# The residual of the last column group is put into PSUM ahead of the tail's matmuls

## The chip, the cores and the metric

The kernel runs on one core of a Trainium2 chip. The metric is the device time in microseconds (us) of one execution. Engines: PE is the matmul engine, DVE the vector engine, ACT the scalar engine, POOL the general one, SP the engine that issues most DMAs. [...]

## What is computed

A trunk of two layers over 256 tokens of width 2048 in float32: gated linear attention, then retention, each with a pre-norm, a SiLU gate, an output projection and a residual add, and a final norm. What matters here is the end: the output projection of the second layer, the residual add and the final norm.

```python
def rms_norm(x, g):
    xf = x.astype(jnp.float32)
    xn = xf * lax.rsqrt(jnp.mean(xf * xf, axis=-1, keepdims=True) + EPS)
    return xn.astype(x.dtype) * g

def reference(...):
    h = x
    for i in range(DEPTH):                       # DEPTH = 2
        ...
            h = h + gla_mixer(rms_norm(h, gla_norm[j]), ...)
        ...
            h = h + retention_mixer(rms_norm(h, ret_norm[j]), ...)   # ends in (o * silu(gate)) @ w_out
    return rms_norm(h, final_norm)
```

## The kernel before

The tokens are two tiles of 128 (t = 0, 1), the 2048 output columns four groups of 512. The weights stream from HBM in blocks of 256 rows by 512 columns (`raw`). Each block is split into a high and a low part (`hi` by ACT at L298, `lo` by DVE at L299), and a float32 product is made of three matmuls (high by high, high by low, low by high): the `mm3` helper, L340 to L342. A projection group is a loop over row blocks that accumulates into one PSUM bank per token tile.

The second half of the last output projection is written out by hand in `out_last` and `out_tail`. Column group 0 comes first. Of group 3 the first four row blocks are done early (`HEAD = 4`), and their sum is added to the residual tile `resid` in SBUF. Then `out_pair` does groups 1 and 2 together, in a scheme with fewer products; its banks are called `rbe_ps`, and its results are joined into `resid` by DVE (`join`, L990 and L992), squared and summed by ACT (`square_sum`, L599) and multiplied by the final norm's weights by DVE (L1005). What is left for `out_tail` is the other four row blocks of group 3, for which the weights are already split and kept.

`out_tail` goes over the token tiles. For tile 0 it issues 24 matmuls of 512 columns into one bank (`tail_ps`). For tile 1 it issues 48 of 256 columns into two banks, so that the first half of the columns is done before the second. Behind each tile stands its epilogue, in halves of 256 columns: DVE adds the PSUM result to the residual (L1150), ACT squares it and sums the squares (L1152), DVE multiplies it by the norm weights (L1154). Then a short chain of small operations (`rsqrt_col`, L1115 to L1120) gives the token's factor, DVE and ACT scale the five column pieces by it (L1168, L1170), and each piece is sent out by a DMA (L1172), issued on SP's queue after a DVE scaling and on ACT's own queue after an ACT scaling.

The order on an engine is set by a scheduler at build time, from data dependences and an estimate of times. `keep(...)` pins an instruction behind the instruction that was traced just before it on the same engine (an ordering, no wait for its end). The last splits, the joins, the squares of the joint pair and the table load at the start of `out_tail` (L1126) are pinned, and so are the tail's matmuls, as `mm3` pins every matmul of a group that does not begin at row block 0:

```python
        pin = keep if begin else lambda x: x
...
    keep(nc.scalar.preload_act_table_set("natural_log_exp_and_others"))
...
                eng = nc.scalar if which == "s" else nc.sync
                eng.dma_start(out[t * P : (t + 1) * P, piece], src)
```

PSUM banks for the accumulators go round in a queue of four (`slots`). When `out_tail` begins, its order is 1, 2, 3, 0: tile 0 gets bank 1, tile 1 banks 2 and 3.

## Time and profile before

| | |
|---|---|
| median of 3 runs | 1374.77 us (1374.18 to 1375.06) |
| profiled execution | 1373.6 us, its span 1371.8 us |
| PE busy | 1361.9 us, 99% of the span |
| DVE busy | 1100.0 us, 80% |
| ACT busy | 846.6 us, 62% |
| mean granted PE clock | 0.998 |

The span runs from the first to the last instruction of the profiled execution; what lies around it is in the time of the execution. A timeline row has the start in us from the span's start, the duration, the engine and the line of the kernel, the operation, "out<-in" by the program's names, the shape, and in brackets how long the engine had been idle before it and what ended that. Matmuls are pipelined: their starts are the reliable column, and the end of a matmul is modelled.

### The profile page before, as it was taken

The page shows a single profiled execution, that of the slowest core. Times are in us where ns is not written, and L with a number is a line of the kernel's source. Part 1 is how long each engine was busy: PE and PEld are TensorE (multiplying, and loading weights), DVE is VectorE, ACT ScalarE, POOL GpSimd, SP SyncE. Part 2 cuts the span into 40 slices and gives each one's busy share as a digit, 9 for nine tenths or more (in the row PEclk, how much of TensorE's full clock was granted, in tenths as well). Part 3 has the DMA queues.
Part 4 walks back from the last instruction along what each step waited for, and adds up shares of the span by engine and source line. Part 5 has one row for each costly group of instructions (what it writes and reads, how often), then busy time and mean ns, then how long its engine had stood idle before and what let it go on. Part 6 is the DMA issues. An engine that isn't in the chain of part 4 may idle for free.

```text
span 1371.8 us, 18375 instructions
## 1 busy us (share of the span) xinstructions
PE 1361.9 (99%) x6564; PEld 1143.5 (83%) x6564; DVE 1100.0 (80%) x1524; ACT 846.6 (62%) x1116; POOL 136.7 (10%) x194
## 2 busy tenths in 40 slices
PE   9999999999999999999999999999999999999997
PEld 8888888888888888888888888888888888888886
DVE  7686795987878896769888888887867897889796
ACT  6576656656567747656666566655546666666565
POOL 1003020110021021001011010100101101010010
PEclk9999999999999999999999999999999999999999
DMA  9755566789658667868897878896798797869773
GB/s 365 257 172 167 174 203 184 158 249 324 192 153 268 205 205 180 314 168 239 271 321 201 256 202 252 207 313 215 174 363 230 234 262 195 262 194 321 236 179 121
DMA packets 84507, 315.03 MB, mean 230 GB/s; under 512 B 9776, under 2 KB 10800, under 8 KB 83136
## 3 DMA queue, kind: packets, MB, share of 16 engines
q1 hardware_dynamic: 67200, 241.63, 50.6%
q0 software_dynamic: 15920, 64.89, 23.7%
q10 hardware_dynamic: 1296, 7.35, 1.5%
q8 instruction: 51, 0.84, 0.2%
q14 instruction: 40, 0.33, 0.1%
HBM read 303.35 MB, written 10.49 MB: 229 GB/s over the span
## 4 chain that ended last, share of the span: by engine, by line
PE 96%; DMA 2%; DVE 1%; issue 1%; ACT 0%; DVEq 0%; POOL 0%; ACTq 0%; POOLq 0%
PE rqk_ps L383 8%; PE re_ps L412 7%; PE re_ps L413 7%; PE re_ps L411 7%; PE rqk_ps L384 4%; PE gqk_ps L383 4%; PE gg_ps L341 3%; PE gv_ps L342 3%; PE gv_ps L341 3%; PE gv_ps L340 3%; PE gg_ps L342 3%; PE gg_ps L340 3%; PE ge_ps L413 2%; PE ge_ps L411 2%; PE ge_ps L412 2%; PE gae_ps L413 2%
## 5 line engine op out<-in xcount | busy, mean ns | idle before, releaser
L299 DVE TENSOR_TENSOR lo<-raw,hi 128x1024 fp32r<-128x1024 f32 (+1 forms) x568 | 687.1, 1219 | 215.6 <-ACT hi L298 206.5
L298 ACT ACTIVATE hi<-raw 128x1024 fp32r<-128x1024 f32 (+1 forms) x568 | 596.1, 1055 | 393.8 <-PE gg_ps L342 49.0
L383 PE MATMUL rqk_ps<-xhl,hi 128*128 128x512 f32 x480 | 162.8, 397 | 0.0
L412 PE MATMUL re_ps<-lo,xhl 128*128 128x512 f32 x352 | 137.4, 390 | 0.3 <-DVE lo L299 0.3
L413 PE MATMUL re_ps<-hi,xhl 128*128 128x512 f32 x352 | 137.1, 390 | 0.0
L310 POOL DMA_DIRECT2D raw<-in_w_all x90 | 78.0, 868 | 555.4 <-DVE lo L299 270.6
L411 PE MATMUL re_ps<-hi,xhl 128*128 128x512 f32 x352 | 132.4, 391 | 0.0
L384 PE MATMUL rqk_ps<-xhl,lo 128*128 128x256 f32 x480 | 122.3, 280 | 0.0
L383 PEld LDWEIGHTS rqk_ps<-xhl,hi 128*128 128x128 f32 x480 | 89.5, 188 | 17.9
L384 PEld LDWEIGHTS rqk_ps<-xhl,lo 128*128 128x128 f32 x480 | 87.5, 189 | 3.4
L412 PEld LDWEIGHTS re_ps<-lo,xhl 128*128 128x128 f32 x352 | 66.1, 188 | 13.9 <-DVE lo L299 0.8
L413 PEld LDWEIGHTS re_ps<-hi,xhl 128*128 128x128 f32 x352 | 66.1, 188 | 13.7
L411 PEld LDWEIGHTS re_ps<-hi,xhl 128*128 128x128 f32 x352 | 66.0, 188 | 13.3
L383 PE MATMUL gqk_ps<-xhl,hi 128*128 128x512 f32 x216 | 76.6, 399 | 0.0
L341 PE MATMUL gg_ps<-lo,xhl 128*128 128x512 f32 x192 | 75.4, 393 | 0.0
L341 PE MATMUL gv_ps<-lo,xhl 128*128 128x512 f32 x192 | 75.2, 392 | 0.0
L340 PE MATMUL gv_ps<-hi,xhl 128*128 128x512 f32 x192 | 75.1, 393 | 0.0
L342 PE MATMUL gv_ps<-hi,xhl 128*128 128x512 f32 x192 | 75.0, 391 | 0.0
L342 PE MATMUL gg_ps<-hi,xhl 128*128 128x512 f32 x192 | 74.9, 390 | 0.0
L340 PE MATMUL gg_ps<-hi,xhl 128*128 128x512 f32 x192 | 74.8, 391 | 0.0
L828 POOL TENSOR_TENSOR s<-s,m 128x64 f32<-128x64 f32 x56 | 36.0, 674 | 232.6 <-DVE m L819 223.3
L384 PE MATMUL gqk_ps<-xhl,lo 128*128 128x256 f32 x216 | 59.0, 280 | 0.0
(434 smaller groups left out, 2654.8 us busy)
## 6 DMA issues: line engine op xcount, KB each, us to landing
raw<-in_w_all SPq DMA_DIRECT2D x449, 512.0 KB, 5.0
raw<-in_w_all POOLq DMA_DIRECT2D x90, 512.0 KB, 6.9
resid<-in_x_n SPq DMA_DIRECT2D x2, 1024.0 KB, 10.0
gg<-in_gn_g POOLq DMA_DIRECT2D x8, 256.0 KB, 4.4
resid_x<-resid ACTq DMA_DIRECT2D x1, 2048.0 KB, 7.9
gb<-in_gn_b POOLq DMA_DIRECT2D x8, 256.0 KB, 5.8
gb_resid<-resid_x POOLq DMA_DIRECT2D x1, 2048.0 KB, 11.1
resid_g<-gb_resid ACTq DMA_DIRECT2D x1, 2048.0 KB, 9.5
```

The lines of the kernel that those rows point to most:

```text
L298: a = nc.scalar.activation(hi[:, sl], src[:, sl], AF.Copy)
L299: b = nc.vector.tensor_tensor(lo[:, sl], src[:, sl], hi[:, sl].bitcast(F32), ALU.subtract)
L310: nc.gpsimd.dma_start(raws[n], block(key), accum_op=ALU.add)
L340: pin(mm(ps, xh, hi[:, q, :], start=kt == begin, stop=False))
L341: pin(mm(ps, xh, lo[:, q, :], start=False, stop=False))
L342: pin(mm(ps, xl, hi[:, q, :], start=False, stop=kt == end - 1))
L383: mm(ps[c], wh, rhs[:, kt, :, :], start=kt == 0, stop=False)
L384: mm(ps[c][:, 0, :], wl, rhs[:, kt, 0, :], start=False, stop=False)
L411: pin(mm(ps, xh, hi[:, q, :], start=start, stop=False, **again))
L412: pin(mm(ps, xh, lo[:, q, :], start=False, stop=False, **again))
L413: pin(mm(ps, xl, hi[:, q, :], start=False, stop=stop, **again))
L828: nc.gpsimd.tensor_tensor(dst, dst, side_of(m[:, li, :], z), ALU.add)
```

## The change

Ahead of each tile's matmuls, ACT copies the residual of the last column group into the banks that the matmuls will use: one copy of 512 columns for tile 0, two of 256 for tile 1, each pinned by `keep`. The first matmul of the group no longer overwrites the bank (`start` only where the row block is 0), so the matmuls add to what was copied. In the epilogue the add on DVE goes, and the square and the multiply read PSUM instead of the residual tile in SBUF. The copies are traced at L1135 of the new kernel; for tile 0 the instruction traced before them on ACT is the table load, for tile 1 it is the last output DMA that tile 0's epilogue issues on ACT's queue.

```diff
@@ mm3
         pin = keep if begin else lambda x: x
-        pin(mm(ps, xh, hi[:, q, :], start=kt == begin, stop=False))
-        pin(mm(ps, xh, lo[:, q, :], start=False, stop=False))
-        pin(mm(ps, xl, hi[:, q, :], start=False, stop=kt == end - 1))
+        onto = {"skip_group_check": True} if begin else {}
+        pin(mm(ps, xh, hi[:, q, :], start=kt == 0, stop=False, **onto))
+        pin(mm(ps, xh, lo[:, q, :], start=False, stop=False, **onto))
+        pin(mm(ps, xl, hi[:, q, :], start=False, stop=kt == end - 1, **onto))
@@ out_tail
             ps = acc(2, f"tail_ps{t}", (P, half)) if t else acc(1, f"tail_ps{t}")
+            for n, p in enumerate(ps):
+                w = half if t else GW
+                keep(nc.scalar.activation(p, cur["resid"][:, t, base + n * w : base + (n + 1) * w], AF.Copy))
             for j in range(HEAD, NSUB):
...
             for n in range(2):
-                dst = cur["resid"][:, t, base + n * half : base + (n + 1) * half]
-                nc.vector.tensor_tensor(dst, ps[n] if t else ps[0][:, n * half : (n + 1) * half], dst, ALU.add)
+                at = slice(n * half, (n + 1) * half)
+                src = ps[n] if t else ps[0][:, at]
                 junk = sg_p.tile([P, half], F32, tag="sg", name="sqj")
-                nc.scalar.activation(junk, dst, AF.Square, accum_out=sq[:, n : n + 1])
-                at = slice(n * half, (n + 1) * half)
-                nc.vector.tensor_tensor(last[:, at], dst, fns[3][:, at], ALU.mult)
+                nc.scalar.activation(junk, src, AF.Square, accum_out=sq[:, n : n + 1])
+                nc.vector.tensor_tensor(last[:, at], src, fns[3][:, at], ALU.mult)
```

## The prediction

> **What bounds the kernel now.** I read the page's head and the chain that ended last first, then the timeline of the last 32 us, because the edit touches nothing before that. "PE" is the matmul engine, "DVE" the vector engine, "ACT" the scalar engine.

> ```profile
> span 1371.8 us, 18375 instructions
> PE 1361.9 (99%) x6564; PEld 1143.5 (83%) x6564; DVE 1100.0 (80%) x1524; ACT 846.6 (62%) x1116; POOL 136.7 (10%) x194
> PE 96%; DMA 2%; DVE 1%; issue 1%; ACT 0%; DVEq 0%; POOL 0%; ACTq 0%; POOLq 0%
> ```

> PE is the bound: it is busy for 99% of the span and is 96% of the chain. ACT has slack (62%), but slack over the span says nothing of the moment at which the new copies run. That moment is in the next rows: the timeline (start, duration, engine, line) where the last joint pair of column groups (rbe_ps) ends and the tail (tail_ps) begins.

> ```profile
> 1352.01 0.39 PE L413 MATMUL rbe_ps<-hi,ogt 128*128 128x512 f32 x1
> 1352.24 0.39 PE L340 MATMUL tail_ps<-xhl,ogt 128*128 128x512 f32 x1
> 1352.26 0.68 DVE L990 TENSOR_TENSOR rb_resid<-rbe_ps,rb_resid 128x512 f32<-128x512 f32 x1
> 1353.04 0.63 ACT L599 ACTIVATE sqj<-rb_resid 128x512 f32<-128x512 f32 x1 [2.68 <-DVE rb_resid L990]
> 1353.79 0.69 DVE L1005 TENSOR_TENSOR rb_resid<-rb_resid,fn 128x512 f32<-128x512 f32 x1 [0.85 <-ACT sqj L599]
> 1354.40 0.68 DVE L990 TENSOR_TENSOR rb_resid<-rbe_ps,rb_resid 128x512 f32<-128x512 f32 x1
> 1355.18 0.63 ACT L599 ACTIVATE sqj<-rb_resid 128x512 f32<-128x512 f32 x1 [1.42 <-DVE pre L1129]
> 1355.72 0.19 ACT L599 ACTIVATION_READ_ACCUMULATOR sqj<-rb_resid 128x1 f32 x1
> 1355.92 1.28 ACT L1126 ACT_TABLE_LOAD   x1
> ```

> Two things are to be seen. PE goes from rbe_ps to tail_ps without a gap (1352.01 to 1352.24, the usual spacing). And ACT is behind it: joins on DVE, squares on ACT and multiplies on DVE wait for one another in turn, so ACT's last square ends at 1355.91 and its table load at 1357.20, when token tile 0's 24 tail matmuls are nearly all issued. Today nobody on PE waits for that.

> The end of token tile 0 and its epilogue, which today lies beside token tile 1's matmuls:

> ```profile
> 1357.45 0.39 PE L342 MATMUL tail_ps<-xhl,ogt 128*128 128x512 f32 x1
> 1357.68 0.28 PE L340 MATMUL tail_ps<-xhl,ogt 128*128 128x256 f32 x1
> 1357.88 0.75 DVE L1150 TENSOR_TENSOR rb_resid<-tail_ps,rb_resid 128x256 f32<-128x256 f32 x2 [1.00 <-PE tail_ps L342]
> 1358.40 0.42 ACT L1152 ACTIVATE sqj<-rb_resid 128x256 f32<-128x256 f32 x1 [1.19 <-DVE rb_resid L1150]
> 1358.55 0.75 DVE L1154 TENSOR_TENSOR last<-rb_resid,fn 128x256 f32<-128x256 f32 x2
> 1359.22 0.20 DVE L1156 TENSOR_SCALAR pre<-sq,pre 128x1 f32<-128x1 f32 x1
> 1359.52 0.29 ACT L1116 ACTIVATE nf_nw<-sq,pre 128x1 f32<-128x1 f32 x1 [0.21 <-DVE pre L1156]
> 1360.64 1.12 ACT L1170 ACTIVATE rb_resid<-rb_resid,fin 128x256 f32<-128x256 f32 x2 [0.59 <-DVE fin L1120]
> 1361.18 0.96 ACTq L1172 DMA_DIRECT2D out<-rb_resid  x2
> ```

> And the end of token tile 1, which sets the end of the kernel:

> ```profile
> 1363.31 0.28 PE L342 MATMUL tail_ps<-xhl,ogt 128*128 128x256 f32 x1
> 1363.71 0.42 DVE L1150 TENSOR_TENSOR rb_resid<-tail_ps,rb_resid 128x256 f32<-128x256 f32 x1
> 1364.16 0.42 ACT L1152 ACTIVATE sqj<-rb_resid 128x256 f32<-128x256 f32 x1 [0.28 <-DVE rb_resid L1150]
> 1367.11 0.41 SPq L1172 DMA_DIRECT2D out<-last  x1
> ```

> **What is removed: four DVE adds (L1150).** Only the last one is on the path to the end. PE ends at 1363.31 + 0.28 = 1363.59, the last square starts at 1364.16. Without the add it can start as soon after PE as the first add does now (1357.45 + 0.39 = 1357.84 to 1357.88, 0.04): at 1363.63. Gain 0.53 us. The two removed in tile 0 shorten its epilogue: the multiplies (1358.55) start 0.67 earlier, at the time of the first add, so L1156 and the Ln (L1116) behind it come 0.67 earlier; the squares then end at about 0.95 after PE, just in time. From PE's end to the end of ACT's work for tile 0, the second DMA issue at 1361.18 + 0.96 = 1362.14, today's 4.30 become 3.63.

> **What is added: three ACT copies, and where they are queued.** Each copy is pinned behind the instruction traced before it on ACT. For tile 0 that is the table load, itself pinned behind the last square of the joint pair. So the copy can't use ACT's idle 2.68 us before 1353.04; it starts at 1357.20. Its price has no row of its own; these are the nearest groups (count, busy us, mean ns):

> ```profile
> L874 ACT ACTIVATE go_ps<-go 128x512 f32<-128x512 f32 x16 | 9.5, 596 | 0.3
> L599 ACT ACTIVATE sqj<-rb_resid 128x512 f32<-128x512 f32 x6 | 3.7, 621 | 4.1 <-DVE rb_resid L990 2.7 <-DVE pre L1129 1.4
> L1152 ACT ACTIVATE sqj<-rb_resid 128x256 f32<-128x256 f32 x4 | 1.7, 414 | 3.1 <-DVE rb_resid L1150 3.1
> L400 ACT ACTIVATE gqk_h<-gqk_ps 128x256 f32<-128x256 f32 x16 | 6.0, 383 | 3.2 <-PE gqk_ps L381 3.0
> ```

> L874 writes PSUM from SBUF at the same size: 0.60 us (0.62 by the next row). With 0.1 us of hand-over (DVE's first add in tile 0 ends some 0.42 after 1357.88, the square starts at 1358.40) PE's first tail matmul starts at 1357.20 + 0.60 + 0.10 = 1357.90 instead of 1352.24: **first stall, +5.66**. Hand-over and copy together could be off by 0.2 either way. Queued behind the waiting matmul are all 72 matmuls of the tail; everything later moves with them. DVE's joins are not delayed, since the rbe_ps matmuls stand ahead of the wait.

> For tile 1 the instruction traced before its two copies is tile 0's second output DMA on ACT's queue. It waits for the scaling (L1170), which waits for the norm, which waits for tile 0's last matmul. So tile 1's matmuls, which today start 0.16 before tile 0's last result (1357.68 against 1357.84), start after tile 0's whole ACT epilogue: 3.63, plus one copy of 256 columns (0.41, or 0.38 by L400), plus 0.10. That is 4.14 after tile 0's end: **second stall, +4.30**. If ACT's DMA issues turned out not to stand in front, it would be about 0.4 less. The second copy runs under the first three matmuls of bank 0 (0.12 apart), about nothing. The output DMAs move with the rest and have the DMA engines to themselves as before: nothing.

> At full clock: 5.66 + 4.30 − 0.53 = **+9.43 us**.

> **The clock after a stall.** PE has no gap of several us in the trace, except at its two ends. The first two rows are the start (20 warm-up matmuls), the others 0.2 us slices after PE's end (columns: length, busy of PE, PEld, DVE, ACT, POOL, then PEclk).

> ```profile
> 1.00 1.65 PE L520 MATMUL warm_ps<-warm 128*128 128x128 f32 x6 [1.00 <-POOL lnone L522]
> 4.15 0.63 PE L520 MATMUL warm_ps<-warm 128*128 128x128 f32 x2
> 4.79 0.50 PE L520 MATMUL warm_ps<-warm 128*128 128x128 f32 x3
> ...
> 1366.40:1366.60 0.20, 0.00 (x0) 0.00 (x0) 0.20 (x2) 0.20 (x1) 0.00 (x0) 1.00 0.00 0
> 1366.60:1366.80 0.20, 0.00 (x0) 0.00 (x0) 0.20 (x1) 0.20 (x1) 0.00 (x0) 0.75 0.00 0
> 1366.80:1367.00 0.20, 0.00 (x0) 0.00 (x0) 0.17 (x1) 0.15 (x1) 0.00 (x0) 0.50 0.00 0
> ```

> Until 4.79 the same matmul takes twice as long as after it (start to start some 0.21 us, then 0.11): PE began at 1.00 and ran 3.8 us at half speed, which loses 1.9 us. At the other end the granted clock falls to 0.50 at about 1366.7, 3.1 us after PE's last result. The stalls leave PE idle for 5.5 us (1352.40 to 1357.90) and 4.1 us. Both are longer than 3.1, so the clock should fall in them, and each restart would lose between nothing and 1.9 us; if the clock needs longer than the start shows, up to about 2.9. I take the whole 1.9 for the first stall and 0.9 for the second, which outlasts 3.1 by only 1 us: **+2.8**, bounds 0 and 5.8.

> [...]

> **Squares and multiplies on one bank.** After the change ACT's square and DVE's multiply both read the PSUM bank, in tile 0 both halves of one bank. Whether they then wait for each other is shown by the transposes, where both engines read two halves of one bank:

> ```profile
> 145.65 0.84 ACT L499 ACTIVATE ogt<-got_tp,smalls 128x256 fp32r<-128x256 f32 x2 [1.73 <-PE got_tp L706]
> 146.16 0.87 DVE L500 SCALAR_TENSOR_TENSOR ogt<-got_tp,smalls,ogt 128x256 fp32r<-128x256 f32 x2 [0.98 <-ACT ogt L499]
> ```

> ACT's second read (to 145.65 + 0.84 = 146.49) overlaps DVE's first (from 146.16) for 0.33 us and neither is stretched: I take nothing, with 0 to 0.8 as bounds. [...] If they were kept apart, that is a rival below.

> **Sum.** +9.43 + 2.8 = +12.2 us. On the profiled execution (1373.6 us with its span of 1371.8, 1.8 us lying around the span) that gives 1385.8 us; on the median of the runs, 1374.77 us, it gives 1387.0 us. The measurement can tell about 0.2%, 2.7 us, from no change.

> **Rivals.**
> (a) The stalls come, but the clock stays at full speed, or falls once and recovers at once. [...] Against: the drop after 3.1 us. Time: 1374.8 + 9.4 = 1384.2 us. Chance 0.13.
> (b) Only the first stall: ACT's stream has tile 1's copies ahead of tile 0's epilogue. It would cost +5.66 + 1.9 − 0.53 = +7.0, 1381.8 us. Against: the copy's pin names the DMA issue, which depends on all of tile 0. Chance 0.05.
> (c) The other side: the edit does what it seems to, the copies run before PE needs the bank (ACT idles for 2.68 us before 1353.04). This decides if the pin to the table load does not hold and the first copy is over by 1352.2. Then only the add goes: −0.53, 1374.2 us, too little to be told from no change. Chance 0.05.
> (d) Reads of one bank are serialized. In tile 0 each half's square and multiply then follow one another; four in a row of 0.41 instead of two side by side delay the second stall's end by up to 0.8: 1387.8 us. Against: the overlap at 146.16. Chance 0.12.

> The forecast, both stalls and a clock that drops, has 0.65.

> **How the numbers follow.** Predicted: 1387.0 us, the likeliest case. Its own bounds: +9.4 (1384.2) with no clock loss, +15.2 (1390.0) with 5.8. Leaving (b) and (c) out (0.10), and the outermost of the hand-overs and of the clock's upper bound, the range is 1383.8 to 1390.2 us. It holds (a), (d) and the forecast. Slower by over 0.2% is the forecast with (a), (b) and (d): 0.95. Within 0.2% is (c) but for 0.01: 0.04. Faster by over 0.2% (2.7 us) needs more than the 0.53 us that is on the path: 0.01.

> **What would show it.** Right: PE's first tail matmul waits some 5.5 us for an ACT copy on L1135 that follows the table load at once; PE waits a second time, some 4 us, for a copy that starts only after the second ACT DMA issue of tile 0; matmul spacing of 0.45 instead of 0.23 for a few us after each; the last square 0.05 after PE. Wrong: tail matmuls at 1352.2 as before (then (c)), tile 1's copies ahead of tile 0's square (then (b)), spacing unchanged behind the stalls (then (a)), squares and multiplies in turn on tile 0 (then (d)).

## The result, and the profile after

The changed kernel takes 1387.98 us (median of 5 runs, 1386.87 to 1390.17) against 1374.77 us (5 runs, 1374.18 to 1375.8): a ratio of 1.0097, 95% interval 1.0082 to 1.0112. That is 13.2 us slower; 12.2 were predicted. The profiled execution took 1386.87 us with a span of 1385.1 us, 13.3 us over the profiled execution of before; it is the fastest of the five.

The timeline of PE in the changed kernel, from the last matmul of the joint pair to the end of the tail (the lines have moved: `mm3` is L341 to L343, the table load L1127, the square L1156, the multiply L1157):

```profile
1351.67 0.39 PE L414 MATMUL rbe_ps<-hi,ogt 128*128 128x512 f32 x1
1357.53 0.80 PE L341 MATMUL tail_ps<-xhl,ogt 128*128 128x512 f32 x1 [5.47 <-ACT tail_ps L1135]
1358.12 0.63 PE L342 MATMUL tail_ps<-tail,ogt 128*128 128x512 f32 x1
1358.55 0.63 PE L343 MATMUL tail_ps<-xhl,ogt 128*128 128x512 f32 x1
...
1364.25 0.39 PE L343 MATMUL tail_ps<-xhl,ogt 128*128 128x512 f32 x1
1369.39 0.58 PE L341 MATMUL tail_ps<-xhl,ogt 128*128 128x256 f32 x1 [4.76 <-ACT tail_ps L1135]
...
1377.19 0.28 PE L343 MATMUL tail_ps<-xhl,ogt 128*128 128x256 f32 x1
```

Both stalls are there and both name the copy: PE idles 5.47 us ahead of tile 0 and 4.76 us ahead of tile 1. Behind the first wait the matmuls of 512 columns start 0.43 us apart (1358.12, 1358.55) instead of 0.23.

ACT's timeline beside it shows what the copies are queued behind:

```profile
1354.84 0.63 ACT L600 ACTIVATE sqj<-rb_resid 128x512 f32<-128x512 f32 x1 [1.42 <-DVE pre L1130]
1355.38 0.19 ACT L600 ACTIVATION_READ_ACCUMULATOR sqj<-rb_resid 128x1 f32 x1
1355.58 1.28 ACT L1127 ACT_TABLE_LOAD   x1
1356.88 0.60 ACT L1135 ACTIVATE tail_ps<-rb_resid 128x512 f32<-128x512 f32 x1
1364.73 0.38 ACT L1156 ACTIVATE sqj<-tail_ps 128x256 f32<-128x256 f32 x1 [7.25 <-PE tail_ps L343]
1365.70 0.38 ACT L1156 ACTIVATE sqj<-tail_ps 128x256 f32<-128x256 f32 x1 [0.49 <-DVE last L1157]
1366.20 0.29 ACT L1117 ACTIVATE nf_nw<-sq,pre 128x1 f32<-128x1 f32 x1
1367.41 1.12 ACT L1173 ACTIVATE rb_resid<-rb_resid,fin 128x256 f32<-128x256 f32 x2 [0.68 <-DVE fin L1121]
1367.95 0.96 ACTq L1175 DMA_DIRECT2D out<-rb_resid  x2
1368.95 0.69 ACT L1135 ACTIVATE tail_ps<-rb_resid 128x256 f32<-128x256 f32 x2 [0.42 <-ACT rb_resid L1173]
```

The first copy starts as soon as the table load ends, and tile 1's copies start 0.04 us after the second DMA issue of tile 0's epilogue ends (1367.95 + 0.96 = 1368.91). One thing is new: tile 0's second square waits 0.49 us for DVE's multiply, though both only read.

The windows of the changed kernel, cut at its clock's steps (length, busy time of PE, of its weight loads PEld, of DVE, ACT and POOL, granted PE clock, then what the DMA moved):

```profile
1357.53:1360.43 2.90, 2.90 (x7) 2.35 (x8) 0.00 (x0) 0.00 (x0) 0.00 (x0) 0.50 0.01 3
1360.43:1364.64 4.21, 4.20 (x19) 3.11 (x17) 0.00 (x0) 0.00 (x0) 0.00 (x0) 1.00 0.00 0
1369.39:1374.09 4.70, 4.70 (x22) 4.70 (x23) 0.00 (x0) 0.26 (x1) 0.00 (x0) 0.50 0.47 165
1374.09:1377.47 3.38, 3.38 (x28) 3.18 (x27) 0.17 (x1) 0.47 (x2) 0.00 (x0) 1.00 0.00 0
```

Tile 0 starts with 2.90 us at half speed and tile 1 with 4.70 us, which loses 1.45 and 2.35 us.

Stage by stage, from the two profiles:

| stage | before | after | difference | predicted |
|---|---|---|---|---|
| last rbe_ps start to first tail start | 0.23 | 5.86 | +5.63 | +5.66 |
| tile 0, first start to last end | 5.60 | 7.11 | +1.51 | +1.9 |
| tile 0's last end to tile 1's first start | −0.16 | 4.75 | +4.91 | +4.30 |
| tile 1, first start to last end | 5.91 | 8.08 | +2.17 | +0.9 |
| PE's end to the last instruction | 8.21 | 7.63 | −0.58 | −0.53 |
| sum | | | +13.64 | +12.2 |

The tail began 0.34 us earlier in the profiled execution of after (1351.67 against 1352.01), which makes 13.3 of the 13.64.

### The profile page after: what moved, and what is told of

The parts are those of the page before. It is cut to its first block, busy times and chain, and to the rows that moved or that the text cites. A ratio compares the mean times of both kernels' runs of the same rounds, so it can differ in the third digit from the quotient of the medians.

```text
span 1385.1 us, 18372 instructions
## 1 busy us (share of the span) xinstructions
PE 1365.8 (99%) x6564; PEld 1146.6 (83%) x6564; DVE 1099.1 (79%) x1520; ACT 848.1 (61%) x1119; POOL 136.8 (10%) x194
## 4 chain that ended last, share of the span: by engine, by line
PE 97%; DVE 1%; DMA 1%; ACT 1%; issue 0%; DVEq 0%; ACTq 0%
PE rqk_ps L384 8%; PE re_ps L412 8%; PE re_ps L414 8%; PE re_ps L413 8%; PE rqk_ps L385 4%; PE gqk_ps L384 4%; PE gg_ps L342 3%; PE gv_ps L343 3%; PE gv_ps L342 3%; PE gv_ps L341 3%; PE gg_ps L343 3%; PE gg_ps L341 3%; PE ge_ps L413 2%; PE ge_ps L414 2%; PE ge_ps L412 2%; PE gae_ps L414 2%
## 5 line engine op out<-in xcount | busy, mean ns | idle before, releaser
L413 PE MATMUL re_ps<-lo,xhl 128*128 128x512 f32 x352 | 137.3, 390 | 0.0
L413 PEld LDWEIGHTS re_ps<-lo,xhl 128*128 128x128 f32 x352 | 66.1, 188 | 13.3
L412 PEld LDWEIGHTS re_ps<-hi,xhl 128*128 128x128 f32 x352 | 66.0, 188 | 13.2
L342 PE MATMUL gg_ps<-lo,xhl 128*128 128x512 f32 x192 | 75.4, 393 | 0.0
L342 PE MATMUL gv_ps<-lo,xhl 128*128 128x512 f32 x192 | 75.2, 392 | 0.0
L341 PE MATMUL gv_ps<-hi,xhl 128*128 128x512 f32 x192 | 75.1, 393 | 0.0
L343 PE MATMUL gv_ps<-hi,xhl 128*128 128x512 f32 x192 | 75.0, 391 | 0.0
L343 PE MATMUL gg_ps<-hi,xhl 128*128 128x512 f32 x192 | 74.9, 390 | 0.0
L341 PE MATMUL gg_ps<-hi,xhl 128*128 128x512 f32 x192 | 74.8, 391 | 0.0
```

The lines of the kernel that those rows point to most:

```text
L341: pin(mm(ps, xh, hi[:, q, :], start=kt == 0, stop=False, **onto))
L342: pin(mm(ps, xh, lo[:, q, :], start=False, stop=False, **onto))
L343: pin(mm(ps, xl, hi[:, q, :], start=False, stop=kt == end - 1, **onto))
L412: pin(mm(ps, xh, hi[:, q, :], start=start, stop=False, **again))
L413: pin(mm(ps, xh, lo[:, q, :], start=False, stop=False, **again))
```

## The experiments

The theory: nothing that the edit adds costs time by itself. What costs is where the copies stand in ACT's stream, because PE waits for them, and the PE clock, which falls while PE waits. Rivals: adding onto data that ACT wrote is slow, or banks and data aren't ready any earlier. The kernel before ran beside the experiments at 1374.1 us (e1 to e4) and 1373.89 us (e6 to e9), medians of 21 runs each; e10's time is that of one execution.

**e1: the copies traced earlier, still pinned.**

```diff
@@ out_pair, ahead of the held-back squares
+            keep(nc.scalar.activation(sides[0][0], cur["resid"][:, 0, 3 * GW :], AF.Copy))
+            keep(nc.scalar.activation(sides[1][0], cur["resid"][:, 1, 3 * GW : 3 * GW + GW // 2], AF.Copy))
@@ out_pair, behind whole(g, 0)
+            keep(nc.scalar.activation(sides[1][1], cur["resid"][:, 1, 3 * GW + GW // 2 :], AF.Copy))
@@ out_tail: the copies there are gone
```

> The copies are traced earlier: into the banks of tile 0 and of tile 1's first half ahead of the held-back squares of the joint pair, into the third bank behind the first square of column group 2; still pinned. Theory (the loss is where the copies stand in ACT's stream, and the clock behind it): no gap on PE, matmul spacing 0.23 and 0.12 as before the change, only the removed add shows: 0.5 to 0.6 us under the kernel before, 1374.2. Rival (adding onto data that ACT wrote, or reading PSUM in the epilogue, costs of itself): matmul spacing still 0.43 behind the copies, and a time of 1377 or more.

Measured: 1374.11 us, ratio 1.0001 (0.9992 to 1.0010). PE has no gap and the spacing is as before the change. ACT's timeline of this run:

```profile
1349.98 0.58 ACT L1053 ACTIVATE tail_ps<-rb_resid 128x512 f32<-128x512 f32 x1
1350.50 0.37 ACT L1054 ACTIVATE tail_ps<-rb_resid 128x256 f32<-128x256 f32 x1
1354.61 0.37 ACT L1062 ACTIVATE tail_ps1b<-rb_resid 128x256 f32<-128x256 f32 x1
```

The same three copies, adds onto PSUM (the memory that the matmuls write here, `tail_ps<-xhl,ogt`) and reads of it cost nothing here. So the 13 us are the place of the copies. The gain of 0.5 to 0.6 doesn't show in the time: from PE's end (1364.53) to the last instruction (1372.3) are 7.8 us, 0.4 less than before, and the runs spread over 2.7 us.

**e4: the pin on the copies taken away, all else as in the change.**

```diff
-                keep(nc.scalar.activation(p, cur["resid"][...], AF.Copy))
+                nc.scalar.activation(p, cur["resid"][...], AF.Copy)
```

> The change without the pin on the three copies, all else as it is. Theory (the pins put the copies behind the table load and behind tile 0's DMAs; data and banks would allow them earlier): the copies run ahead of 1352, no gaps, 1374.2 us. Rival (banks or the residual are not ready earlier, the pins change nothing): 1388 us.

Measured: 1373.65 us, ratio 0.9997 (0.9988 to 1.0006). ACT's timeline:

```profile
1342.12 0.58 ACT L1135 ACTIVATE tail_ps<-rb_resid 128x512 f32<-128x512 f32 x1
1344.84 0.39 ACT L1135 ACTIVATE tail_ps<-rb_resid 128x256 f32<-128x256 f32 x1 [1.15 <-DVE rb_resid L991]
1354.55 0.37 ACT L1135 ACTIVATE tail_ps<-rb_resid 128x256 f32<-128x256 f32 x1
```

Without the pin the first copy runs some ten us ahead of PE's first tail matmul (1353.07), and the second runs as soon as a join on DVE is done that it waits for. PE has no gap. The copies and the adding onto them cost nothing; the place that `keep` holds them to costs 13 us.

**e2: all three copies directly behind the table load.**

```diff
+        seeded = [acc(1, "tail_ps0"), acc(2, "tail_ps1", (P, half))]
+        for t, ps in enumerate(seeded):
+            ...                                   # the pinned copies, ahead of the loop over t
         for t in range(2):
```

> All three copies stand directly behind the table load, so tile 1's no longer stand behind tile 0's output DMAs. Theory: only the first stall is left, 5.6 us, with 0 to 2.9 us for the clock behind it, less 0.6 for the add: 1379.8 to 1382.7 us, most likely 1381.3; tile 1's matmuls follow tile 0's without a gap. Rival (tile 1 waits for something else of tile 0, its bank or its reads): the second gap of 4.8 us stays and the time is 1388.

Measured: 1381.82 us (1380.25 to 1382.44), ratio 1.0055 (1.0043 to 1.0068). The second gap is gone, the first is unchanged:

```profile
1357.55 1.21 ACT L1132 ACTIVATE tail_ps<-rb_resid 128x512 f32<-128x512 f32 x3
1358.20 0.80 PE L341 MATMUL tail_ps<-xhl,ogt 128*128 128x512 f32 x1 [5.48 <-ACT tail_ps L1132]
...
1365.96 0.39 PE L343 MATMUL tail_ps<-xhl,ogt 128*128 128x512 f32 x1
1366.18 0.28 PE L341 MATMUL tail_ps<-xhl,ogt 128*128 128x256 f32 x1
```

So the second stall is tile 0's epilogue on ACT, and nothing else of tile 0.

**e3: PE kept at work in both stalls.**

```diff
+            idle = lev_p.tile([P, GW], F32, tag="lev", name=f"idle{t}")
+            some = splits[state["sub"]] if t == 0 else kept[0]
+            for i in range((23, 17)[t]):
+                keep(mm(idle, ogt[:, 0, 0, 0:P], some[0][:, 0, :], start=True, stop=True))
```

> The change as it is, with 23 and 17 extra matmuls of 512 columns (result unused) ahead of tile 0's and tile 1's tail matmuls, so that PE works for 5.2 and 3.9 us of the two stalls. Theory (slow matmuls behind a stall are the granted clock, which falls when PE idles): the stalls stay, the spacing behind them is 0.23 and 0.12, and 3 to 4 us of the 13.2 come back: 1384.2 us. Rival (matmuls are slow because they add onto a bank that ACT has written): spacing stays 0.43 for some us, 1388 us or more.

Measured: 1384.09 us (1384.02 to 1385.13), ratio 1.0075 (1.0061 to 1.0088). That is 10.0 us over the kernel before, where the change is 13.2: PE does more, and 3.2 us come back. The 10.0 us are what the stage table gives without the two matmul stages (5.63 + 4.91 − 0.58 = 9.96). The windows behind the two waits, at full clock:

```profile
1358.08:1363.83 5.75, 5.75 (x25) 4.77 (x26) 0.00 (x0) 0.00 (x0) 0.00 (x0) 1.00 0.00 1
1368.59:1374.60 6.01, 6.00 (x48) 5.80 (x48) 0.17 (x1) 0.73 (x3) 0.00 (x0) 1.00 0.39 131
```

The copies and the adds onto them are the same as in the change, so the slow matmuls were the clock's, and the clock fell because PE idled.

**e7: the table load behind tile 0's copy.**

```diff
-        keep(nc.scalar.preload_act_table_set("natural_log_exp_and_others"))
...                                               # in the loop, behind the copies
+            if t == 0:
+                keep(nc.scalar.preload_act_table_set("natural_log_exp_and_others"))
```

> The change as it is, but the table load is traced behind tile 0's copy instead of ahead of it. Theory (PE's first wait is the length of ACT's stream ahead of the copy): the first stall is shorter by the load, 1.28 us, so 4.2 us of idle PE instead of 5.5, and the load runs beside tile 0's matmuls; 1386.5 us, between 1384.5 and 1388 by what the clock does. Rival (the copy waits for the last square of column group 2 or a bank): the stall stays at 5.5.

Measured: 1387.34 us (1386.14 to 1388.72), ratio 1.0096 (1.0082 to 1.0109). That is 13.4 us over the kernel before, as much as the change's 13.2, though the stall got shorter as expected. PE's first wait, and the windows behind both waits:

```profile
1357.05 0.80 PE L341 MATMUL tail_ps<-xhl,ogt 128*128 128x512 f32 x1 [4.04 <-ACT tail_ps L1134]
```

```profile
1357.05:1362.80 5.75, 5.75 (x14) 4.49 (x15) 0.40 (x3) 1.25 (x1) 0.00 (x0) 0.50 0.00 1
1370.27:1376.46 6.19, 6.19 (x29) 6.19 (x30) 0.00 (x0) 0.25 (x1) 0.00 (x0) 0.50 0.36 125
```

The wait is 1.4 us shorter (4.04 against 5.47; 1.28 was expected), but in this execution the clock stayed at half for 5.75 and 6.19 us behind the stalls, 6.0 us lost instead of 3.8. By these profiles the length of the stall alone doesn't set how long it stays there: ahead of tile 1 PE was idle for 4.76 us in both kernels, and behind that the clock was at half for 6.19 us here and for 4.70 in the change. How often the runs without a profile lost as much isn't known.

**e6: both squares traced ahead of both multiplies, and e10: tile 0 in two banks.**

```diff
@@ e6
-                nc.vector.tensor_tensor(last[:, at], src, fns[3][:, at], ALU.mult)
...                                               # both multiplies in a loop of their own behind the squares
@@ e10
-            ps = acc(2, f"tail_ps{t}", (P, half)) if t else acc(1, f"tail_ps{t}")
+            ps = acc(2, f"tail_ps{t}", (P, half))
...                                               # tile 0 goes through tile 1's matmul loop
```

> The change as it is, but in each epilogue both squares are traced ahead of both multiplies. In the changed kernel's profile tile 0's square, multiply, square, multiply run one behind the other, though they only read the bank, and the norm's Ln starts 1.56 us after PE's last tail matmul. Theory (ACT and DVE are never let onto one PSUM bank at the same time, and the order square, multiply, square makes ACT wait): the two squares follow each other, Ln starts about 1.15 after PE, the second stall is 0.4 shorter, and the multiplies still don't overlap a square of tile 0. Time 0.4 us under the change, 1387.2, with the clock's spread of about 1 us. Rival (the reads may overlap, and the second square was late for another reason): multiplies run beside squares, or Ln stays at 1.56.

Measured: 1388.35 us (1387.67 to 1389.01); 0.4 us can't be seen in that time. In the profile Ln, the logarithm on L1117, comes 0.97 us after PE's end (1.15 was expected), and the second stall is 4.49 us, 0.26 shorter than in the change (0.4 was expected). DVE's multiplies (1366.25) start behind the second square's end (1366.13), but they also stand behind other work on DVE there, so this run alone doesn't tell whether they had to.

> The change as it is, but tile 0 uses two banks of 256 columns like tile 1 (two copies and 48 matmuls of 256 columns, halves in turn to the end, so that they are done 0.36 us apart). Theory (the order square, multiply, square, multiply in tile 0 came from the two halves lying in one bank): the second square starts some 0.05 after PE without waiting for DVE, and beside the first multiply; from PE's end to ACT's scaling 1.9 us instead of 2.77, the second stall 3.9 instead of 4.75. Rival (ACT waits for DVE for another reason): the second square still starts behind the first multiply's end, scaling at 2.4 us or later.

Measured: ACT's and DVE's timelines around tile 0's end (PE's last result at 1366.15):

```profile
1365.89 0.38 ACT L1152 ACTIVATE sqj<-tail_ps 128x256 f32<-128x256 f32 x1 [7.46 <-PE tail_ps L343]
1366.26 0.38 ACT L1152 ACTIVATE sqj<-tail_ps 128x256 f32<-128x256 f32 x1
1368.24 1.12 ACT L1169 ACTIVATE rb_resid<-rb_resid,fin 128x256 f32<-128x256 f32 x2 [0.68 <-DVE fin L1121]
```

```profile
1366.39 0.42 DVE L1153 TENSOR_TENSOR last<-tail_ps,fn 128x256 f32<-128x256 f32 x1 [8.99 <-ACT sqj L1152]
```

With the halves in two banks the second square follows the first at once and runs beside the first multiply. ACT's scaling comes 2.09 us after PE instead of 2.77, and the stall is 4.07 us instead of 4.75 (1.9 and 3.9 were expected). Not all of these 0.68 us is the bank: the first half is also done earlier, so that its square starts 0.26 us ahead of PE's last result, where in the change it starts 0.09 us behind it. The time, 1388.36 us, is one execution and its clock loss is part of it.

**e8: only tile 1, unpinned; e9: e4 with both squares first.**

```diff
@@ e8
+            for n in range(2 if t else 0):
+                nc.scalar.activation(ps[n], cur["resid"][:, t, ...], AF.Copy)
...                                               # tile 0 keeps its start flag and its adds
```

> Only tile 1 gets its residual through PSUM, its two copies unpinned; tile 0 is as before the change. Theory (only the last add is on the path to the end): no stall, the last square 0.04 after PE as with all three copies unpinned, 0.3 to 0.5 us under the kernel before: 1373.7. Rival (tile 0's adds are worth something too): 1374.1 or more, as before.

> All three copies unpinned, and both squares traced ahead of both multiplies. With the copies unpinned the profile shows 1.90 us from the last square to ACT's scaling, against 1.67 before the change, because the last half's multiply stands ahead of two steps of the norm on DVE. Theory: squares first take 0.2 of that back; from PE's end to the last instruction 7.6 us, against 7.8 unpinned and 8.2 before; 1373.5 us, not to be told from the unpinned kernel by the time alone. Rival: 7.8 us as unpinned.

Measured: e8 1373.46 us, ratio 0.9994 (0.9986 to 1.0003); e9 1372.99 us, ratio 0.9995 (0.9986 to 1.0004). Neither can be told from the kernel before by its time. By the profiles, PE's end to the last instruction is 7.82 us in e8 (1363.75 to 1371.57), 7.83 us in e4 (1364.42 to 1372.24) and 7.63 us in e9 (1363.27 to 1370.90), against 8.21 before. In e9 ACT's scaling starts 1.72 us behind the last square:

```profile
1363.30 0.38 ACT L1156 ACTIVATE sqj<-tail_ps 128x256 f32<-128x256 f32 x1 [0.24 <-PE tail_ps L343]
1365.02 1.12 ACT L1175 ACTIVATE rb_resid<-rb_resid,fin 128x256 f32<-128x256 f32 x2 [0.68 <-DVE fin L1121]
```

So by one profile each, tile 1 alone brings the same 0.39 us as all three copies do in e4, and the squares first another 0.20 us. The idea behind the edit is worth 0.4 to 0.6 us in the stage that it touches, some 0.03 to 0.04% of the kernel, less than these runs can resolve.

## Why the prediction was right, and where its sizes were off

**The first stall** came as worked out: 5.63 against 5.66. The copy took 0.60, as the row of the nearest write to PSUM had it (596 ns), and the hand-over to PE 0.05 instead of 0.10. e4 without the pin and e1 with the pin at an earlier place have no stall, so it comes from the place that the pin holds the copy to.

**The gain at the end** came too: the last square starts 0.04 us after PE (1377.19 + 0.28 = 1377.47 to 1377.51), and the stage is 0.58 shorter, against 0.53.

**The second stall** had the right cause (e2) and a wrong size, 4.91 against 4.30. The step that failed is "squares and multiplies on one bank": I took nothing, and the mechanism of rival (d) came, at 0.6 of its 0.8. From PE's end to the end of ACT's work the prediction had 3.63 us; it is 4.27 (1364.64 to 1368.91), and 0.49 us of the difference is the second square's wait for DVE's multiply. My evidence was a pair of rows in which two reads of got_tp on ACT overlap a read on DVE. Such rows are merged and leave buffer numbers out: by the order of ACT's instructions the two reads in a row are of two transposes' banks, and only the third goes back to the first bank. The list of waits of the kernel before had the answer (waited in total, times, longest):

```profile
ACT ogt L499 <- DVE ogt L500: 4.9, 5, 1.7
```

ACT's second read of a bank waits there for DVE's read of the other half. The runs of the change agree: 0.49 us of waiting with both halves in one bank, none with two (e10). In the kernel before, the same square and multiply read one tile in SBUF and did overlap (ACT from 1358.40 for 0.42, DVE from 1358.55), so sharing a tile is not enough to make them wait. Whether in PSUM the bank or the program's tile is the unit can't be told from these runs, since each bank held one tile.

**The clock** was the second term mis-sized: +3.7 in the profile (1.51 and 2.17) against +2.8. That it falls in both stalls was right; e3 shows it is the idle time. The loss per restart was taken from the start of the kernel, 1.9 us, and half of that for the second stall. In the stalls of the change, e2, e6, e7 and e10 the clock stayed at half for 2.90 to 6.19 us after the restart, 1.45 to 3.1 us lost, in the second stall as much as in the first. The start of the kernel was one draw, not the upper end: in the change's profile the warm-up matmuls start 0.21 us apart until 5.21, 4.2 us after PE's first instruction at 1.00, where before the change they did until 4.79, 3.8 us after it. The upper bound of 2.9 us for a restart was my estimate without a row behind it: no run shows it, and e7's second restart lost 3.1.

**The runs** lie between 1386.87 and 1390.17, a spread of 3.3 us against 1.6 for the kernel before in the same comparison, and 1.1 for e3: the mean granted clock is 0.994 or 0.995 in every run of the change and 0.998 or 0.999 in every run of e3, so each run of the change lost time to the clock. That the total came within 1 us is in part luck. Both misses, +0.6 and +0.9 us, went the same way, and what the clock takes differs by run: 3.7 us in the change's profile, 6.0 in e7's. The range held because its bounds for the clock were wide. Rivals (a), (b) and (c) did not come about, though (c) is what e4 made happen.

## What to carry to other kernels

Before an operation is put ahead of a busy engine's work, ask what stands in front of it on its own engine at that moment: the share of busy time (ACT's 62%) says nothing of it, the timeline does. An order that is pinned "behind what was traced before" is as good as the place in the text where it stands; here one word at that place cost 13 us around a copy of 0.6. And a stall of the matmul engine can cost more than its length: in these runs PE stood still nine times for 4.0 to 5.5 us, and each time the matmuls behind it started at half speed.

## What the runs showed of the hardware that I had not expected

In the change's profile the half-speed stretch, counted from the fall of the clock, lasted 3.41 us the first time (1357.02 to 1360.43) and 6.83 us, twice as long, the second time (1367.26 to 1374.09), though the second stall was the shorter one (4.76 us against 5.47). In e2 it was about 6.8 us, an estimate from its windows: the granted clock averages 0.85 over 1352.73 to 1358.20, so it was at half for 1.64 of those 5.47 us, and it stayed there for 5.20 us more, until 1363.40. The rows are the change's two stalls up to the fall of the clock and after it:

```profile
1352.06:1357.02 4.96, 0.00 (x1) 0.00 (x0) 2.97 (x8) 2.87 (x6) 0.00 (x0) 1.00 0.00 0
1357.02:1357.53 0.51, 0.00 (x0) 0.00 (x1) 0.00 (x0) 0.46 (x1) 0.00 (x0) 0.50 0.00 0
1364.64:1367.26 2.62, 0.00 (x0) 0.00 (x0) 1.62 (x7) 1.45 (x6) 0.00 (x0) 1.00 0.00 0
1367.26:1369.39 2.13, 0.00 (x0) 0.00 (x0) 1.26 (x4) 1.56 (x4) 0.00 (x0) 0.50 0.37 129
```

PE had not been idle all the while before the clock fell: in the 3.41 us ahead of the fall it had still worked for 0.78 us in the change's second stall (1363.85 to 1367.26), and for 1.45 us at the end of e4:

```profile
1362.97:1366.39 3.42, 1.45 (x13) 1.24 (x11) 1.76 (x8) 1.48 (x7) 0.00 (x0) 1.00 0.80 278
1366.39:1369.80 3.41, 0.00 (x0) 0.00 (x0) 1.12 (x3) 1.09 (x2) 0.00 (x0) 0.50 0.69 246
```
